# A feed-forward's gate and up products as seven block products instead of eight

## The chip, the cores and the metric

One Trainium2 chip, and of it one core. The metric is the time of the program on the device in microseconds. TensorE (the profile's PE) multiplies and accumulates in PSUM, VectorE (DVE) and ScalarE (ACT) work on elements, GpSimd (POOL) had next to no work so far, and SyncE (SP) issues DMAs.

## The reference

Three transformer layers run over 512 tokens of width 1024 in fp32. Each ends with a gated feed-forward of width 2816. The change concerns that of the third layer:

```python
u = rmsnorm(h, norm2_w[l]) * (1.0 + sc2) + sh2
ff = (jax.nn.silu(u @ w_ffn_gate[l]) * (u @ w_ffn_up[l])) @ w_ffn_down[l]
h = h + g2 * ff
```

## The kernel before

Activations are transposed: 128 features on the partitions, 512 tokens along the free axis, so that 1024 features are eight k-tiles. An fp32 product is made of three passes. Each operand is split into a high part (rounded, by a copy on ScalarE) and a low part (value minus high part, by VectorE); `mm3` issues high x high, high x low and low x high. A matmul is 128 weights wide and takes 512 tokens, or 256 where the work is done in token halves.

Weights are one stream of 128x128 tiles in the order in which they are used (`weight_plan`). Sixteen tiles are a unit of 1 MB, loaded by SP into one of `RAWBUFS` = 2 buffers `wraw` (`load_unit`, `load_ahead`); half a unit is a half-unit, split in one piece of 128x1024 into one of three pairs `whi`/`wlo` (`prep_half`). `wtile` gives a product its tile and keeps two half-units prepared ahead.

The feed-forward `ffn` (tag F2 for the third layer, 22 f-tiles of 128) works in two halves of eleven f-tiles. For each f-tile it makes gate and up (2 x 8 weight tiles, 48 matmuls), each in a PSUM bank; `act_chain` takes silu(gate) x up and splits the result into `ph`, `pl`. Then follow the eleven-tile down products of all eight outputs. In F2 the first f-tile, and the gate of the second, are made by `gemm_wide` in two token halves, because the normalized inputs `xh`, `xl` come out of `explicit_x` one half after the other. For every third k-tile `explicit_x` takes another path: the scaling on ScalarE and the low part on GpSimd (line 264).

The order of the instructions comes from a planner that runs when the kernel is built. Each stretch of work is a generator with a priority; `Core` keeps a model time for each engine, and `Core.run` always goes on with the generator that is due at TensorE's model time. Its prices (a matmul n/2400 us, a DMA by its size) only decide the order in which instructions stand in each engine's queue. On the chip every engine takes its own queue in that order and waits for what it reads and overwrites.

Of the kernel before, what the change touches and what calls it, by code (L numbers as in the profile page):

```python
# [17 lines left out]
P = 128  # L18
T = 512
# [15 lines left out]
RAWBUFS = 2  # L35
# [21 lines left out]
def weight_plan():  # L57
    tiles = []
    gains = {}

# [23 lines left out]
    def ffn(g, u, d, wide=False):  # L84
        for half in range(2):
            for f in range(half * HALF, (half + 1) * HALF):
                if wide and f == 0:
                    wide_k((g, 0), (u, 0), (g, P))
                    continue
                if not wide or f != 1:  # L90
                    form_a(g, [f])
                form_a(u, [f])
            form_a(d, range(8), nk=HALF, k0=half * HALF)

# [9 lines left out]
    while len(tiles) % UNIT:  # L104
        tiles.append(None)
# [9 lines left out]
    ffn("w_gate1", "w_up1", "w_down1")  # L115
    for what, h in ORDER_IN:
# [15 lines left out]
    ffn("w_ffn_gate_2", "w_ffn_up_2", "w_ffn_down_2", True)  # L132
    return tiles, gains


PLAN, GAINS = weight_plan()
# [25 lines left out]
class Core:  # L162
# [140 lines left out]

    def now(self):
        return self.pe_t + LAT
# [78 lines left out]
def kernel(ctx: ExitStack, tc, wst, wada, xT, vec, cst, rope, bias1, alibi, hmask, out):  # L384
# [50 lines left out]

    def raise_(hu):
# [34 lines left out]
    def load_ahead():  # L471

        while state["loaded"] < NUNITS:
            old = 2 * (state["loaded"] - RAWBUFS)
            if any(x >= state["prepped"] or highs[x] or lows[x] for x in range(max(old, 0), old + 2)):
                break
            load_unit()

    def prep_half(split=1):
# [5 lines left out]
        hi = wpool.tile([P, 1024], FR, name="whi", bufs=3)  # L485
        lo = wpool.tile([P, 1024], FR, name="wlo", bufs=3)
# [17 lines left out]
    def wtile(i, n=1, look=2, top=NHALF - 1):  # L504
        hu = i // 8
        while state["prepped"] <= min(hu + look, top):
            if state["prepped"] // 2 not in raw:
# [27 lines left out]
    def mm3(o, w, x, first, last, n=T):  # L535
        E.mm(o, w[0], x[0], first, False, n=n)
        E.mm(o, w[0], x[1], False, False, n=n)
        E.mm(o, w[1], x[0], False, last, n=n)
# [18 lines left out]
    def gemm_wide(banks, i0, hook=None, need=None, wide=False, halves=None):  # L557

        ny = len(banks)
        for t, cols in enumerate(halves or (FULL,)):  # L560
            top = (i0 + ny * KT - 1) // 8 if halves and not t else NHALF - 1
            for k in range(KT):
# [9 lines left out]
                yield  # L572

# [289 lines left out]
    def ffn(tag, pool, explicit, upd, split=False):  # L863
# [24 lines left out]
        for half in range(2):  # L888
# [14 lines left out]
            last = KT - 2 if half and split else KT  # L903
            for m in range(last):
# [485 lines left out]

    def explicit_x(bank, gain, shift, tag, t):
        c = HALVES[t]
        n = T // 2
        for k in range(KT):
            u = tmp.tile([P, n], FT, name="ut", bufs=3)
            if k % 3 == POOLK:
# [426 lines left out]
    def main():  # L1823
# [14 lines left out]
        with tc.tile_pool(name="ffn1", bufs=1) as pool:  # L1838
# [5 lines left out]
            yield from ffn("F1", pool, False, down("L2", x=False, gain2="norm_final"), split=True)  # L1844
        with tc.tile_pool(name="layer2", bufs=1) as pool:
# [4 lines left out]
        with tc.tile_pool(name="ffn2", bufs=1) as pool:  # L1850
# [3 lines left out]
            yield from ffn("F2", pool, True, down("Z", x=False, scale=mod_col(5)), split=True)  # L1854
# [79 lines left out]
```

## Time and profile before

| | us |
|---|---|
| median of 3 runs | 1929.25 (1928.06 to 1930.36) |
| the profiled execution's own time | 1928.12 |
| its span, first to last instruction | 1926.3 |
| TensorE busy | 1909.9 |
| VectorE busy | 1138.1 |
| ScalarE busy | 842.6 |
| GpSimd busy | 7.0 |

The span and all rows come from the one profiled execution. A busy time is the sum of an engine's instructions; matmuls overlap in it, so that the start-to-start distance says more than the length of one. The granted TensorE clock was 0.999 of full speed over the span.

### The profile page before, as it was taken

Reading aid. Unit: us, or ns where it says so; the run is one execution under the profiler, and the core shown is the slowest. Engines: PE = TensorE matmul, PEld = TensorE weight load, DVE = VectorE, ACT = ScalarE, POOL = GpSimd, SP = SyncE. Lnnn points to the kernel's source line nnn. Section 1 sums busy time; section 2 is a strip of 40 time slices with the busy share of each in tenths; the row PEclk is TensorE's granted clock in tenths of the full one; section 3 lists DMA queues with packets and bytes.
Section 4 is the critical chain, followed back from the end, with each engine's and each line's share of the span. In section 5 each row is a group of like instructions: output and inputs, shape, how many; then the busy total and the mean of one; then the engine's idle time right before and its main releaser. Section 6 shows DMA issues by size and latency. Waiting matters only on the chain.

```text
span 1926.3 us, 23731 instructions
## 1 busy us (share of the span) xinstructions
PE 1909.9 (99%) x9331; PEld 1593.4 (83%) x9331; DVE 1138.1 (59%) x1946; ACT 842.6 (44%) x1361; POOL 7.0 (0%) x14
## 2 busy tenths in 40 slices
PE   9999999999999999999999999999999999999998
PEld 6888888888888878888888888898888888888887
DVE  5877866655665578887543344475777563333334
ACT  4876743322333466665332233352555452212233
POOL 0000000000000000000000000000000000000000
PEclk9999999999999999999999999999999999999999
DMA  6333224544542344431322232322121222222321
GB/s 195 100 88 99 77 88 173 203 182 175 188 173 88 124 134 129 129 116 66 110 95 102 88 109 88 109 81 99 55 81 47 88 88 88 100 97 90 108 88 66
DMA packets 48303, 211.94 MB, mean 110 GB/s; under 512 B 7056, under 2 KB 10304, under 8 KB 29248
## 3 DMA queue, kind: packets, MB, share of 16 engines
q1 hardware_dynamic: 48192, 210.43, 32.5%
q8 instruction: 73, 1.20, 0.3%
q14 instruction: 38, 0.31, 0.0%
HBM read 186.26 MB, written 2.10 MB: 98 GB/s over the span
## 4 chain that ended last, share of the span: by engine, by line
PE 96%; DVE 2%; DMA 1%; ACT 1%; issue 0%; SPq 0%; POOLq 0%; POOL 0%; DVEq 0%; ACTq 0%
PE ps L229 94%; PE ps L235 2%; DMA wraw<-wst 0%; DMA h<-xT 0%; DVE wlo L260 0%; DVE xl L276 0%; ACT xh L242 0%; DVE ut L276 0%; SPq L298 0%; ACT whi L242 0%; DVE h L260 0%; ACT sqh L242 0%; ACT ut L242 0%; DVE h L276 0%; DVE e L276 0%
## 5 line engine op out<-in xcount | busy, mean ns | idle before, releaser
L229 PE MATMUL ps<-xh,whi 128*128 128x512 f32 (+1 forms) x1856 | 722.4, 389 | 3.5 <-ACT whi L242 1.8
L229 PE MATMUL ps<-xl,whi 128*128 128x512 f32 (+1 forms) x1856 | 711.4, 383 | 2.2 <-POOL xl L264 1.9
L229 PE MATMUL ps<-xh,wlo 128*128 128x512 f32 (+1 forms) x1856 | 710.8, 383 | 0.5 <-DVE wlo L260 0.5
L242 ACT ACTIVATE whi<-wraw 128x1024 fp32r<-128x1024 f32 (+1 forms) x280 | 290.8, 1039 | 603.4 <-PE ps L229 559.0
L260 DVE TENSOR_TENSOR wlo<-wraw,whi 128x1024 fp32r<-128x1024 f32 (+1 forms) x280 | 335.6, 1199 | 326.3 <-ACT whi L242 325.6
L229 PEld LDWEIGHTS ps<-xh,whi 128*128 128x128 f32 x1856 | 349.3, 188 | 73.5 <-ACT whi L242 3.3
L229 PEld LDWEIGHTS ps<-xh,wlo 128*128 128x128 f32 x1856 | 348.9, 188 | 70.3 <-DVE wlo L260 1.1
L229 PEld LDWEIGHTS ps<-xl,whi 128*128 128x128 f32 x1856 | 349.4, 188 | 69.2 <-DVE xl L276 3.0
L229 PE MATMUL ps<-ph,whi 128*128 128x512 f32 (+1 forms) x572 | 214.1, 374 | 0.0
L229 PE MATMUL ps<-pl,whi 128*128 128x512 f32 (+1 forms) x572 | 213.2, 373 | 0.0
L229 PE MATMUL ps<-ph,wlo 128*128 128x512 f32 (+1 forms) x572 | 213.2, 373 | 0.0
L229 PEld LDWEIGHTS ps<-ph,whi 128*128 128x128 f32 x572 | 107.7, 188 | 19.1
L229 PEld LDWEIGHTS ps<-ph,wlo 128*128 128x128 f32 x572 | 107.7, 188 | 18.9
L229 PEld LDWEIGHTS ps<-pl,whi 128*128 128x128 f32 x572 | 107.7, 188 | 18.8
L260 DVE TENSOR_TENSOR fu<-ps,rb 128x512 f32<-128x512 f32 x44 | 30.4, 691 | 95.8 <-PE ps L229 95.8
L260 DVE TENSOR_TENSOR h<-ps,h 128x512 f32<-128x512 f32 (+1 forms) x82 | 49.7, 621 | 60.6 <-PE ps L229 58.9
L242 ACT ACTIVATE fs<-fg 128x512 f32<-128x512 f32 x44 | 27.8, 631 | 91.1 <-DVE fg L260 91.1
L260 DVE TENSOR_TENSOR fs<-ps,fs 128x512 f32<-128x512 f32 x22 | 15.2, 692 | 70.2 <-PE ps L229 69.5
L242 ACT ACTIVATE ph<-fs 128x512 fp32r<-128x512 f32 x66 | 41.7, 632 | 28.4 <-DVE fs L260 28.4
L276 DVE SCALAR_TENSOR_TENSOR adacc<-adaw,sc,adacc 128x1024 f32<-128x1024 f32 x42 | 53.7, 1279 | 0.0
L242 ACT ACTIVATE e<-e 128x1024 f32<-128x1024 f32 (+1 forms) x48 | 41.3, 906 | 21.1 <-DVE e L269 21.0
L242 ACT ACTIVATE s<-s,md 128x256 f32<-128x256 f32 (+3 forms) x80 | 45.9, 585 | 9.9 <-DVE md L269 8.5
(211 smaller groups left out, 1976.4 us busy)
## 6 DMA issues: line engine op xcount, KB each, us to landing
wraw<-wst SPq DMA_DIRECT2D x148, 1024.0 KB, 4.8
adaw<-wada SPq DMA_DIRECT2D x48, 512.0 KB, 5.7
qhh<-hin SPq DMA_DIRECT2D x32, 128.0 KB, 2.4
rfs<-rf SPq DMA_DIRECT2D x64, 64.0 KB, 2.0
khh<-rf SPq DMA_DIRECT2D x32, 128.0 KB, 2.4
h<-xT SPq DMA_DIRECT2D x8, 256.0 KB, 5.2
kst<-hin SPq DMA_DIRECT2D x16, 128.0 KB, 2.4
kst<-qkf SPq DMA_DIRECT2D x16, 128.0 KB, 2.4
```

Source lines behind the costliest of these rows:

```text
L229: self.nc.tensor.matmul(out, lhsT, rhs, start=start, stop=stop, skip_group_check=not group)
L235: self.nc.tensor.transpose(out, in_, ident)
L242: self.nc.scalar.activation(out, in_, func, **kw)
L260: self.nc.vector.tensor_tensor(out, a, b, op)
L276: self.nc.vector.scalar_tensor_tensor(out, a, s, b, op0, op1)
```

## The change

For f-tiles 2 to 10 and 11 to 21 of F2, gate and up of one f-tile are one product of two by two blocks: the weights by rows (gate, up) and by halves of the inputs (k-tiles 0 to 3, 4 to 7), the inputs by those halves and by halves of the tokens (c1, c2). Eight block products of 4 k-tiles become seven (Strassen's scheme in Winograd's form, the up row with its sign turned), each 4 k-tiles x 3 passes of 256 tokens. Tile by tile one unit of 16 weight tiles holds `a11`, `a12` (gate) and `a21`, `a22` (up).

- The products need weight sums: S1 = a21 + a22, S3 = a21 + a11, S2 = a11 + S1, S4 = a12 + S2. GpSimd makes them with DMAs that add to their target (`add_dma`): S1 in a buffer `s1` (three of them; SP loads a21 from HBM, a DMA from HBM adds a22), the others in the raw unit itself, in place. S2 overwrites a11 and S4 overwrites a12, so these must be split first. All seven blocks (512 wide) are then split one by one, in the order of the products, into a ring of ten slots: the six halves of the three pairs and four more (`split_highs`, `split_lows`).
- The inputs need sums as well (`blocks`), once: values of the first token half by a copying and an adding DMA, differences by VectorE, then four more splits for each of four pairs of k-tiles.
- A chain of ScalarE and VectorE operations on 256 tokens (`chain`) takes partial results out of PSUM between the products.
- A raw unit is loaded again only when all seven blocks of the tile in it are split; the third raw buffer is for the whole kernel. The down weights are filled up to a whole unit.
- In F2 `explicit_x` now has one path for all k-tiles, on VectorE and ScalarE, and leaves its values in buffers for `blocks`.

```diff
-RAWBUFS = 2
+RAWBUFS = 3
...
+                if seven and f > 1:
+                    sevens.append(len(tiles) // UNIT)
...
+    def add_dma(self, out, a, sbuf=True):
+        self.nc.gpsimd.dma_start(out, a, accum_op=OP.add)
+        t = max(self.pool_t, self._ready("pool_t", [out], [a] if sbuf else [])) + 1.0
+        self.pool_t = t
+        self._done("pool_d", [out], [a] if sbuf else [], t + DMALAT + 0.7)
...
+    hi_slots = wpool.tile([P, 6, 512], FR, name="whi")
+    lo_slots = wpool.tile([P, 6, 512], FR, name="wlo")
...
+            if old >= 0 and old // 2 in sums_of:
+                break
             load_unit()
...
+            if x > hu and (any(taken[2 * state["pair"] + y] for y in range(2)) or
+                           (x // 2 not in raw and state["loaded"] > 1 and state["loaded"] - 2 in sums_of)):
+                break
...
+    def steps_of(n):
+        steps = [(x, f) for f in range(EARLY) for x in ("a11", "a12")]
+        steps += [(x, f) for x in ("s1", "s2", "s3") for f in range(EARLY)]
+        steps += [(x, f) for f in range(EARLY - 1) for x in ("a22", "s4")]
+        for f in range(EARLY, n - 1):
+            steps += [("a11", f), ("a12", f), ("s1", f), ("s2", f), ("a22", f - 1), ("s4", f - 1), ("s3", f)]
+        f = n - 1
+        steps += [("a11", f), ("a12", f), ("s1", f), ("s2", f), ("a22", f - 1), ("s3", f), ("s4", f - 1), ("a22", f),
+                  ("s4", f)]
+        return steps
...
+    def sums(u0):
...
+        E.spawn(loads(), 899)
+        yield from first(0)
+        for f in range(g["n"]):
+            u = u0 + f
+            if f + 1 < g["n"]:
+                yield from first(f + 1)
...
+            b = [raw[u][:, i * 512:(i + 1) * 512] for i in range(4)]
+            yield from got(*(f"W{u}{x}" for x in (("a11", "a12") if f else ())))
...
+            yield from add(u, b[2], b[0], "S3")
+            yield from add(u, b[0], g["s1"][u], "S2")
+            yield from add(u, b[1], b[0], "S4")
...
+    def split_highs(u0):
...
+        for i, (name, f) in enumerate(g["steps"][2:], 2):
+            u, s = u0 + f, ring[i % len(ring)]
...
+            if taken[s]:
+                yield lambda: not taken[s]
+            taken[s] = True
...
+            g["lows"].append((name, f, E.act(hi, src, AF.Copy)))
...
+    def seven(u0, name, f, out, x, fresh):
...
+        for j in range(4):
+            c = slice(j * P, (j + 1) * P)
+            a, b = yield from x(j)
+            yield from E.there(hi[:, c], lo[:, c], a, b)
+            mm3(out, (hi[:, c], lo[:, c]), (a, b), fresh and j == 0, True, T // 2, False)
+            yield
+        taken[g["slot"][name, f]] = None
...
+        def blocks(j):
+            b = [value[j][:, x, :] for x in range(2)]
+            for x in range(2):
+                yield from E.get(f"{tag}x{j + 4 * x}_0")
+                E.dma(b[x], xh[:, j + 4 * x, c1].bitcast(FT), 128, sbuf=True)
+                yield E._ready("pool_t", [b[x]], [])
+                E.add_dma(b[x], xl[:, j + 4 * x, c1].bitcast(FT))
...
+            E.stt(e, z1, ds, z0, OP.add, OP.subtract, n=n)
...
+            q = b[0]
+            d = E.add_dma(q, e)
...
+            yield E.tt(v, q, b[1], OP.subtract, n=n)
...
+        def chain(half, u, f, a, r5):
+            r = ps[:, a, c1]
+            yield from E.get(f"W{u}pa12")
...
+            d = E.act(g[:, c1], r, AF.Copy, n=n)
+            yield d
+            d = E.tt(g[:, c1], ps[:, a, c2], g[:, c1], OP.add, n=n)
+            E.set(f"W{u}c1", d)
+            yield d
+            E.act(g[:, c1], g[:, c1], AF.Silu, n=n)
+            yield from E.get(f"W{u}ps2")
+            E.set(f"W{u}c2", E.act(g[:, c2], r, AF.Copy, n=n))
+            yield from E.get(f"W{u}ps3")
+            d = E.act(v, r, AF.Copy, scale=-1.0, n=n)
...
+            for name, f in groups[u0]["steps"]:
...
+                before = {"s2": "c1", "s3": "c2", "a22": "c3", "s4": "c4"}.get(name)
+                if before:
+                    yield from E.get(f"W{u}{before}")
...
-            if k % 3 == POOLK:
+            if k % 3 == POOLK and tag != "F2":
...
-            yield from ffn("F2", pool, True, down("Z", x=False, scale=mod_col(5)), split=True)
+            yield from ffn_seven("F2", pool, True, down("Z", x=False, scale=mod_col(5)), split=True)
...
-    nc = bacc.Bacc("TRN2", target_bir_lowering=False, num_devices=1)
+    nc = bacc.Bacc("TRN2", target_bir_lowering=False, num_devices=1, dynamic_dma_scratch_size=2048)
```

`EARLY` is 2, so a group begins with two tiles side by side. The first group has 63 steps, the second 77; step i uses slot i modulo 10. The ring begins with the pair that holds the first tile's a11 and a12, then come the four extra slots, then the other two pairs, of which the next half-unit to be prepared takes the first (steps 6 and 7 modulo 10). The values of `explicit_x` are kept in the buffers that later hold `ph` and `pl`.

## Rows read from the trace of the kernel before

**Rows 1.** The page's first part: busy time, share of the span, number of instructions

```profile
span 1926.3 us, 23731 instructions
...
PE 1909.9 (99%) x9331; PEld 1593.4 (83%) x9331; DVE 1138.1 (59%) x1946; ACT 842.6 (44%) x1361; POOL 7.0 (0%) x14
```

**Rows 2.** The page's fourth part: chain that ended last, by engine, by line

```profile
PE 96%; DVE 2%; DMA 1%; ACT 1%; issue 0%; SPq 0%; POOLq 0%; POOL 0%; DVEq 0%; ACTq 0%
PE ps L229 94%; PE ps L235 2%; DMA wraw<-wst 0%; DMA h<-xT 0%; DVE wlo L260 0%; DVE xl L276 0%; ACT xh L242 0%; DVE ut L276 0%; SPq L298 0%; ACT whi L242 0%; DVE h L260 0%; ACT sqh L242 0%; ACT ut L242 0%; DVE h L276 0%; DVE e L276 0%
```

**Rows 3.** Windows over F2: length, then each engine's busy time and instructions

```profile
core 0: us, PE busy (x) PEld busy (x) DVE busy (x) ACT busy (x) POOL busy (x), PEclk, DMA share, GB/s
1546.00:1556.00 10.00, 9.50 (x71) 8.40 (x70) 9.31 (x20) 6.73 (x15) 0.78 (x1) 1.00 0.31 107
1556.00:1566.00 10.00, 9.69 (x81) 9.49 (x80) 7.34 (x21) 6.17 (x14) 1.46 (x2) 1.00 0.00 0
1566.00:1576.00 10.00, 9.57 (x62) 8.56 (x62) 7.05 (x10) 6.78 (x11) 0.88 (x1) 1.00 0.36 120
1576.00:1586.00 10.00, 10.00 (x46) 8.28 (x45) 3.74 (x4) 3.20 (x4) 0.00 (x0) 1.00 0.27 98
1586.00:1596.00 10.00, 10.00 (x46) 8.29 (x45) 3.74 (x4) 3.20 (x4) 0.00 (x0) 1.00 0.26 100
...
1800.00:1900.00 100.00, 100.00 (x446) 82.93 (x445) 37.15 (x40) 33.01 (x45) 0.00 (x0) 1.00 0.25 84
```

**Rows 4.** TensorE in order of time, 1892 to 1905 us: start, length, instruction

```profile
1892.63 0.39 PE L229 MATMUL ps<-pl,whi 128*128 128x512 f32 x1
...
1899.20 0.28 PE L229 MATMUL ps<-ph,whi 128*128 128x256 f32 x1
...
1905.19 0.28 PE L229 MATMUL ps<-ph,wlo 128*128 128x256 f32 x1
```

**Rows 5.** VectorE and ScalarE in order of time, 1587 to 1599 us

```profile
1587.73 1.06 ACT L242 ACTIVATE whi<-wraw 128x1024 fp32r<-128x1024 f32 x1 [3.84 <-PE ps L229]
1588.03 0.69 DVE L260 TENSOR_TENSOR fs<-ps,fs 128x512 f32<-128x512 f32 x1 [3.36 <-PE ps L229]
1588.76 0.63 ACT L242 ACTIVATE ph<-fs 128x512 fp32r<-128x512 f32 x1
1589.97 0.68 DVE L260 TENSOR_TENSOR pl<-fs,ph 128x512 fp32r<-128x512 f32 x1
1594.33 1.23 DVE L260 TENSOR_TENSOR wlo<-wraw,whi 128x1024 fp32r<-128x1024 f32 x1 [3.67 <-ACT whi L242]
1598.91 0.69 DVE L260 TENSOR_TENSOR fs<-ps,fs 128x512 f32<-128x512 f32 x1 [3.36 <-PE ps L229]
```

**Rows 6.** VectorE and ScalarE in order of time, pieces of 256 tokens, 1561 to 1563 us

```profile
1561.11 0.48 DVE L276 SCALAR_TENSOR_TENSOR xl<-ut,mod,xh 128x256 fp32r<-128x256 f32 x1 [0.19 <-ACT xh L242]
1561.52 0.42 DVE L260 TENSOR_TENSOR ut<-ps,h 128x256 f32<-128x256 f32 x1
1562.03 0.60 ACT L242 ACTIVATE ut<-ut,mod,gv 128x256 f32<-128x256 f32 x1 [0.95 <-DVE ut L260]
1562.66 0.42 ACT L242 ACTIVATE xh<-ut 128x256 fp32r<-128x256 f32 x1
```

**Rows 7.** The page's sixth part, DMA issues: KB of one, median us to landing

```profile
adaw<-wada SPq DMA_DIRECT2D x48, 512.0 KB, 5.7
...
out<-h SPq DMA_DIRECT2D x8, 256.0 KB, 2.2
...
khh<-khh SPq DMA_DIRECT2D x8, 128.0 KB, 5.6
al<-alibi SPq DMA_DIRECT2D x4, 256.0 KB, 5.1
```

**Rows 8.** SP's queue in order of time, the shortest issues

```profile
10.65 0.33 SPq L298 DMA_DIRECT2D wraw<-wst  x1
```

**Rows 9.** GpSimd in order of time, the longest of its subtractions

```profile
1567.26 0.88 POOL L264 TENSOR_TENSOR xl<-ut,xh 128x256 fp32r<-128x256 f32 x1 [3.30 <-ACT xh L242]
```

**Rows 10.** The chain that ended last, in order of time, 1564 to 1580 us

```profile
1564.24 0.40 DVE ut L276
1564.65 0.02 issue
1564.67 0.51 ACT xh L242
1565.18 0.95 ACT whi L242
1566.13 0.55 ACT ut L242
1566.68 0.02 issue
1566.70 0.43 ACT xh L242
...
1567.24 0.92 POOLq L1929
1568.15 0.04 issue
1568.19 12.02 PE ps L229 x64
```

More of the change, by code (lines that the diff above doesn't have):

```diff
@@ L82, in out_proj, with fill, ffn @@
                     tiles.append((name, k * P, m * P))
-    def ffn(g, u, d, wide=False):
+    def fill():
+        while len(tiles) % UNIT:
+            tiles.append(None)
+    def ffn(g, u, d, wide=False, seven=False):
         for half in range(2):
@@ L93, in ffn @@
             form_a(d, range(8), nk=HALF, k0=half * HALF)
+            if seven:
+                fill()
     for p in range(8):
@@ L103, in weight_plan @@
     ffn("w_gate0", "w_up0", "w_down0")
-    while len(tiles) % UNIT:
-        tiles.append(None)
+    fill()
     for p in range(8):
@@ L115, in weight_plan @@
     ffn("w_gate1", "w_up1", "w_down1")
+    fill()
     for what, h in ORDER_IN:
@@ L434 @@
     quiet, by_hand = [], {0, 1}
+    hi_slots = wpool.tile([P, 6, 512], FR, name="whi")
+    lo_slots = wpool.tile([P, 6, 512], FR, name="wlo")
+    slots = [(hi_slots[:, i, :], lo_slots[:, i, :]) for i in range(6)]
+    taken = [None] * 6
+    state["pair"] = 0
+    sums_of = set(SEVENS)
     def raise_(hu):
@@ new lines, in open_group, with block, begin_group @@
+    def open_group(u):
+        n = 1
+        while u + n in SEVENS and n < HALF:
+            n += 1
+        for x in range(n):
+            group_of[u + x] = u
+        groups[u] = dict(n=n, steps=steps_of(n), s1={}, lows=[], slot={}, pool=None, ring=None)
+    def block(u, name):
+        g = groups[group_of[u]]
+        if name == "s1":
+            return g["s1"][u]
+        o = BLOCK[name] * 512
+        return raw[u][:, o:o + 512]
+    def begin_group(u, pool, more):
+        yield lambda: u in raw
+        if u not in group_of:
+            open_group(u)
+        g = groups[u]
+        g["pool"] = pool
+        E.spawn(sums(u), 901)
+        yield lambda: state["prepped"] == 2 * u + 1
+        first = 2 * ((state["pair"] - 1) % 3)
+        g["ring"] = [first, first + 1, *more, *((first + x) % 6 for x in range(2, 6))]
+        for x in range(6):
+            taken[x] = True
+        for x in range(2):
+            g["slot"]["a11" if x == 0 else "a12", 0] = first + x
+        for x in range(state["prepped"], 2 * (u + g["n"])):
+            highs[x] = lows[x] = []
+        state["prepped"] = 2 * (u + g["n"])
+        E.spawn(split_highs(u), 902)
+        E.spawn(split_lows(u), 903)
@@ new lines, in split_lows @@
+    def split_lows(u0):
+        g = groups[u0]
+        left = {}
+        for name, f in g["steps"][2:]:
+            left[f] = left.get(f, 0) + 1
+        for _ in g["steps"][2:]:
+            if not g["lows"]:
+                yield lambda: g["lows"]
+            name, f, d = g["lows"].pop(0)
+            u = u0 + f
+            hi, lo = slots[g["slot"][name, f]]
+            t = max(E.dve_t - SLACKD, d)
+            if t > E.pe_t:
+                yield t
+            E.set(f"W{u}{name}")
+            E.set(f"W{u}{name}x", E.tt(lo, block(u, name), hi.bitcast(FT), OP.subtract))
+            left[f] -= 1
+            if not left[f]:
+                sums_of.discard(u)
+                load_ahead()
@@ new lines, in seven @@
+    def seven(u0, name, f, out, x, fresh):
+        g, u = groups[u0], u0 + f
+        if (name, f) in g["steps"][:2]:
+            hi, lo = wtile(u * UNIT + BLOCK[name] * 4, 4, look=0)
+        else:
+            yield from E.get(f"W{u}{name}x")
+            hi, lo = slots[g["slot"][name, f]]
+        for j in range(4):
[5 more added lines that the diff above has]
+        taken[g["slot"][name, f]] = None
@@ L903, in ffn @@
             last = KT - 2 if half and split else KT
+            for m in range(last):
+                b = yield from E.alloc()
+                hook = (lambda k: E.set(f"{tag}d{k}", E.now())) if m == KT - 1 else None
+                yield from gemm_a(b[0], take(HALF), lambda k: (ph[k], pl[k]), nk=HALF,
+                                  need=f"{tag}p{half}_" if m == 0 else None, hook=hook)
+                E.spawn(upd(m, b[0], half), 3)
+            if last == KT:
+                continue
+            i = take((KT - last) * HALF)
```

219 lines of the change are left out of this document (208 added, 11 removed).

## Prediction

> **What bounds the kernel now.** I read the page's first part, the chain that ended last, and then a table of windows over the last feed-forward (F2, from about 1548 us on). TensorE is busy 99% of the span [rows 1], and 96% of the chain is TensorE [rows 2]. The windows say what lies beside it in the gate and up products: in 1586 to 1596 us TensorE is full, VectorE has 3.74 of 10 us, ScalarE 3.20, GpSimd nothing, and the DMA engines are busy 0.26 [rows 3]. So a matmul that goes away is time gained, until one of those four fills up; how near each comes is the question.
>
> The next view is TensorE's order in time where the kernel itself goes from 512 to 256 columns. From 1892.63 to 1899.20 us stand 29 matmuls of 512 columns: 6.57/29 = 0.2266 us each. From 1899.20 to 1905.19 us stand 50 of 256: 5.99/50 = 0.1198 us [rows 4]. Half the columns cost more than half the time (0.1133). An f-tile (16 weight tiles, three passes, 48 matmuls) is then 48 x 0.2266 = 10.88 us, and VectorE's product of gate and up returns after 1598.91 - 1588.03 = 10.88 us [rows 5]. Nothing else sets the pace there.
>
> **The products.** Twenty f-tiles go from 48 wide matmuls to 7 x 4 x 3 = 84 narrow ones: 84 x 0.1198 = 10.06 us against 10.88, 0.81 us each, **-16.2 us** in all. The columns alone fall by one eighth (1.36 us a tile, 27 us); the step of a narrow matmul takes the rest. The Trainium skill (TensorE: Matmul & The Clock Gate, Back-to-back issue gap) gives N / 2.4 + 2.5 ns; by it a tile would go from 10.36 to 9.17 us and the sum would be 23.7 us. The rows differ from it by 11 to 13 ns a matmul, and the rows decide.
>
> **Splitting the weights.** Four blocks of 512 become seven. ScalarE: 7 x 0.63 for the high parts, 0.63 for the result's, five pieces of 256 at 0.42 to 0.60 [rows 5, 6], about 7.3 us in 10.06. VectorE: 7 x 0.68, 0.68, five pieces of 0.42 to 0.48, about 7.7 us. Both stay under TensorE's 10.06 us, which hides them: **0 us**. If something held VectorE for 2.4 us in every tile, the cover would be gone, and each tenth of a microsecond beyond would cost 2 us over twenty tiles.
>
> **Sums of the weights.** GpSimd, idle until now [rows 1], issues four accumulating DMAs of 256 KB a tile: S1 of the next tile, then S3, S2, S4. S2 overwrites what S3 reads, and S4 reads what S2 writes, so each of the two waits stands at the head of GpSimd's queue, with the next tile's S1 and S3 behind it. With T from its turn to its landing and i for an issue that waits for nothing, the queue goes round in 2T + 2i. The trace has no accumulating DMA. The nearest transfers: 256 KB with nothing beside it lands in 2.2 us; 256 KB and 128 KB behind other loads in 5.1 and 5.6; 512 KB among its like in 5.7 [rows 7]. An issue: 0.33 us on SP at the least [rows 8], 0.88 if it takes GpSimd as long as its longest subtraction [rows 9]. Bounds: 2 x 2.2 + 2 x 0.33 = 5.1 us and 2 x 5.7 + 2 x 0.88 = 13.2 us. Loads will run beside these transfers for about a third of the time, so I take T = 2.2 + (5.6 - 2.2)/3 = 3.3, and 0.7 for reading the target as well as the source (256 KB at the rate below): 4.0; with i = 0.8 the round is 9.6 us, under 10.06: **0 us**, by a margin of 0.5. At the upper end it costs (13.2 - 10.06) x 20 = 63 us, less the lead. The lead is some 4 us in each of the two groups: with ten slots a tile's first block can be split nine steps ahead, S2's product comes three steps after that block, and of these 12 x 1.44 = 17.2 us two splits of 1.3 and two T of 4.0 take 10.6, the queue's other two issues and the fixed order of the splits part of the rest. So +55 us at worst.
>
> **DMA engines.** A tile's 1.05 MB now uses 0.26 to 0.27 of 10 us, 2.7 us of all sixteen engines [rows 3]. The new tile loads 1.25 times that (the second half of the up weights twice), 3.4 us, and adds as much again as one load. If an added byte costs the engines one copied byte, the tile uses 6.1 us; twice, 8.8; three times, 11.5 against 10.06. I take twice, the target being read too: hidden below the 10.06 us, +21 us at three times (1.44 x 20 less the 8 us of lead). The Trainium skill (DMA: Bandwidth & Descriptors, Issuing engines are not separate DMA queues) says that DMAs from any engine run on the same sixteen and interleave. With engines of their own the adds would leave 3.4 us here and the rival of full engines would fall away; no row has two queues at work, and I count them on the same sixteen.
>
> **The start of F2.** The sums of the inputs are new: per pair of k-tiles three additions and four low halves on VectorE (3 x 0.46 + 4 x 0.45 = 3.2 us, 12.7 in all), four copies on ScalarE, and 8 plain and 12 accumulating DMAs. The normalization's third-tile path leaves ScalarE and GpSimd for VectorE: four pieces, 0.55 us more each. VectorE already has 9.31, 7.34 and 7.05 us in the three windows from 1546 us on, and TensorE waits there for the inputs [rows 3, 10]. The moved pieces take away ScalarE, GpSimd and their hand-overs (3.5 us from the ready sum at 1564.67 to TensorE's start at 1568.19 [rows 10]), about what VectorE's extra 2.2 us give back. Until S2's input is wanted, some 14 us after the second half of the inputs is there plus the blocks before it, VectorE has nearly as much to do as time, and a third of the upper bound is my choice: **+3 us** (-1 to +8.6: the hand-overs alone, or all 12.7 + 2.2 us less the 6.3 that VectorE has idle in those windows).
>
> **The down projections.** During a group nothing prefetches the down weights, as the slots are taken; the first 1,024-wide piece is split when the group ends. In the second group the last of the 77 steps uses a slot of that very pair (77th step, ring of ten, seventh slot), so ScalarE's 1.06 and VectorE's 1.23 us [rows 5] come after TensorE's last read: 2.2 us. In the first group (63 steps) the pair is free, but queued behind the last tile's chain: 1 us. **+3.2 us** (0, if the low part hides under the first two matmuls and the queue is short, to 4.6, both groups in full). Nothing else hides it; before, the split lay two pieces ahead.
>
> **Hand-overs in PSUM.** S2's product overwrites the bank part that ScalarE must have copied (0.42 us); the S1 product, 12 x 0.1198 = 1.44 us, is the cover. If the copy queues behind a split (0.63) it still fits; behind two (1.68) each tile loses 0.24: **+1 us** (0 to 4.8).
>
> **Elsewhere.** A third raw buffer lets SP load earlier through the whole kernel, and the padding adds 1 MB. In the steady stretch loads use a quarter of the engines [rows 3], which hides the padding, and SP's queue has 0% of the chain [rows 2]: 0 (-2 to +2, a tenth of a percent of the span, which such a share can hide).
>
> Sum: -16.2 + 3 + 3.2 + 1 = -9.0 us on a profiled execution of 1928.12 us, 1919.1. The median of the runs shown stands 1.1 us above that execution: **1920.3 us**.
>
> **Rivals.** *The queue of sums sets the pace* (slower): place, GpSimd's queue at S2 and S4; for it, transfers that share the engines take 5.1 to 5.7 us [rows 7]; against it, the free one takes 2.2. With T = 5.1 the round is 11.8: 1.74 x 20 - 8 = +27, so 1947 us. It decides from the point where 20 (2T + 2i - 10.06) - 8 = 9, a round of 10.9 us or T = 4.7. The Trainium skill (DMA: Bandwidth & Descriptors, Rules for kernel authors) says that a DMA which reads what another wrote must wait for its semaphore; by that rule T counts twice, as above. The same page's formula (Anatomy of one DMA), 2.0 us plus bytes over 436 GB/s, would give T = 2.6 and a round of 6.8 us, as an estimate, for a plain copy. *The DMA engines fill up*: at three bytes for one, 1941 us; the shares before leave 0.73 free, which speaks against it. *The gain is eaten*: the start at +8.6, the down projections at +4.6 and the hand-overs at +4.8 give +18.0 against -16.2, 1931 us, no change; for it, two engines at three quarters and VectorE's full windows. *No stall at all*: -16.2 alone, 1913 us.
>
> **How the numbers follow.** My forecast has 0.52, no stall 0.08, the gain eaten 0.14, the queue 0.17, the DMA engines 0.09. What this measurement can tell from no change is 0.2%, 3.9 us. Faster: the first two, 0.60. Slower: queue and engines, save 0.01 near the turning point, 0.25. The same: 0.15. The range takes in no stall (less 2 for the rest of the kernel) and the queue at T = 5.1: 1911 to 1948. The forecast's own range is 1915 to 1925.
>
> **What would show it.** Right: in the windows of the groups 84 matmuls every 10.1 us, narrow steps at 0.12 us, ScalarE and VectorE near 0.75, GpSimd's sums landing before the split that reads them. Wrong: TensorE idle in every tile, released by ScalarE or VectorE behind a DMA (the queue); landings that lengthen with the engines' share near 1 (the engines); idle only where a group begins or ends (terms of start and down projections mis-sized). A first F2 product much later than now would condemn the third buffer or the moved normalization.

## The result, and the profile after

The changed kernel takes **2017.78 us** (median of 4 runs, 2017.08 to 2018.56) against 1928.65 us (4 runs, 1926.09 to 1930.36): ratio 1.0463, 95% interval 1.0445 to 1.0482, **slower by 4.6%** where I forecast 1920.3. The profiled execution has a span of 2016.7 us, 90.4 more than before.

The page's first part, which answers to [rows 1]: TensorE is busy 96% of a longer span, GpSimd 4%.

```profile
PE 1930.0 (96%) x10051; PEld 1643.7 (82%) x10051; DVE 1210.6 (60%) x2160; ACT 904.9 (45%) x1551; POOL 84.8 (4%) x102
```

Next the stages of the last feed-forward, as windows cut where TensorE's operands change. The columns are those of [rows 3]; the lines are the changed kernel's end of the wide products, first group (9 tiles), first down projection, second group (11 tiles), and the rest.

```profile
1571.40:1584.40 13.00, 10.16 (x41) 8.31 (x40) 12.38 (x29) 9.92 (x23) 6.44 (x8) 0.74 0.76 143
1584.40:1717.50 133.10, 101.87 (x757) 100.04 (x755) 59.19 (x114) 52.91 (x114) 25.48 (x29) 0.91 0.61 143
1717.50:1778.90 61.40, 60.84 (x264) 49.59 (x265) 23.18 (x26) 15.08 (x18) 4.99 (x7) 1.00 0.43 135
1778.90:1943.10 164.20, 130.29 (x925) 127.64 (x923) 71.38 (x136) 63.91 (x136) 33.71 (x39) 0.86 0.64 147
1943.10:2016.70 73.60, 64.23 (x350) 55.15 (x350) 31.67 (x55) 26.00 (x43) 0.00 (x0) 0.96 0.21 72
```

And the same stages of the kernel before, with its nine and eleven wide tiles:

```profile
1571.40:1576.80 5.40, 5.40 (x26) 4.48 (x25) 2.69 (x4) 2.76 (x5) 0.00 (x0) 1.00 0.28 76
1576.80:1674.80 98.00, 98.00 (x434) 81.13 (x433) 33.70 (x36) 28.47 (x36) 0.00 (x0) 1.00 0.28 100
1674.80:1734.60 59.80, 59.80 (x265) 49.54 (x264) 19.75 (x20) 12.21 (x12) 0.00 (x0) 1.00 0.27 95
1734.60:1854.30 119.70, 119.70 (x529) 99.10 (x529) 40.63 (x43) 34.08 (x43) 0.00 (x0) 1.00 0.28 97
1854.30:1926.30 72.00, 63.45 (x351) 55.18 (x349) 29.34 (x52) 24.81 (x41) 0.00 (x0) 0.97 0.21 74
```

The reader is to see where the 90 us lie: +7.6 ahead of the first group, **+35.1 and +44.5 in the two groups**, +1.6 and +1.6 in the down projections. Up to the last pieces of the normalized input nothing differs: TensorE's wait for a low part of the second half ends within a microsecond of before (1567.37 against 1568.19 us). TensorE, which was full in both groups, now is not: the nine tiles hold 756 narrow matmuls, 756 x 0.1198 = 90.6 us; TensorE is busy 101.9 and idle 31.2. In the second group 924 matmuls are 110.7 us; it is busy 130.3 and idle 33.9. So of the 96 us beyond the bare products 65 are idle time and some 31 are matmuls that ran slower than 0.1198: the granted clock is 0.91 and 0.86 there, against 1.00 before. All of the first group's idle time lies in eight waits, about one for each tile, for partial sums `fs` out of PSUM (us in total, times, longest):

```profile
PE ps L238 <- ACT fs L251: 17.9, 4, 6.1
PE ps L238 <- DVE fs L269: 13.2, 4, 4.7
```

Then GpSimd in order of time over one tile and the beginning of the next. `wraw<-s` is S2, `s<-wst` S1, and of the two `wraw<-wraw` the first is S4, the second S3 of the next tile. The length is the issue's own.

```profile
1604.60 0.86 POOL L315 DMA_DIRECT2D wraw<-wraw  x1 [3.94 <-DMA wraw<-s]
1605.14 1.22 POOL L315 DMA_DIRECT2D s<-wst  x1
1605.67 1.57 POOL L315 DMA_DIRECT2D wraw<-wraw  x1
1615.65 0.86 POOL L315 DMA_DIRECT2D wraw<-s  x1 [8.40 <-issue]
1620.55 0.86 POOL L315 DMA_DIRECT2D wraw<-wraw  x1 [4.04 <-issue]
1621.10 1.21 POOL L315 DMA_DIRECT2D s<-wst  x1
1621.63 1.58 POOL L315 DMA_DIRECT2D wraw<-wraw  x1
1631.80 0.87 POOL L315 DMA_DIRECT2D wraw<-s  x1 [8.59 <-DMA wraw<-wraw]
```

From one S2 to the next are 16.15 us here (14.8 on the mean: 133.1/9). Between them stand two waits of different size: about 4 us from S2 to S4, and over 8 from S3 to the next S2. S3 is issued third: S4 and S1 are on their way when it starts. And SP issues the 1 MB load of a later tile right behind the three, which then runs beside them:

```profile
1606.95 0.33 SPq L307 DMA_DIRECT2D wraw<-wst  x1
```

The landings of 1600 to 1680 us (median from issue) say the same; S2 is the one that goes alone:

```profile
wraw<-wraw POOLq DMA_DIRECT2D x10, 256.0 KB, 6.7
wraw<-s POOLq DMA_DIRECT2D x6, 256.0 KB, 3.3
s<-wst POOLq DMA_DIRECT2D x5, 256.0 KB, 8.2
```

The three that were issued from 1604.60 on landed after 3.9, 6.8 and 9.4 us: one after another, some 3.3 us apart. How this reaches TensorE is seen on ScalarE and TensorE in order of time:

```profile
1613.06 0.38 ACT L251 ACTIVATE fs<-ps 128x256 f32<-128x256 f32 x1 [1.77 <-PE ps L238]
1619.91 2.19 ACT L251 ACTIVATE whx<-wraw 128x512 fp32r<-128x512 f32 x4 [6.47 <-DMA wraw<-s]
1622.01 1.13 ACT L251 ACTIVATE whi<-wraw 128x512 fp32r<-128x512 f32 x2
```
```profile
1622.25 0.28 PE L238 MATMUL ps<-xh,wlo 128*128 128x256 f32 x1
1627.20 0.58 PE L238 MATMUL ps<-th,whx 128*128 128x256 f32 x1 [4.67 <-DVE fs L269]
1627.58 0.42 PE L238 MATMUL ps<-tl,whx 128*128 128x256 f32 x1
1627.80 0.42 PE L238 MATMUL ps<-th,wlx 128*128 128x256 f32 x1
```

ScalarE waits 6.47 us for S2's landing (1615.65 + 4.2), with six more splits and the copies out of PSUM queued behind; then TensorE waits 4.67 us for a sum that VectorE could make only after ScalarE's late copy. The name at the wait is VectorE, the cause is the DMA two engines behind it. After the wait TensorE's steps are 0.21 us, not 0.12: the granted clock is 0.50 of full in 1626 to 1630 us, which is the 1.2 GHz level, after 4.7 us of idling.

### The profile page after: what moved, and what is told of

The parts are those of the page before. It is cut to its first block, busy times and chain, and to the rows that moved or that the text cites. A ratio compares the mean times of both kernels' runs of the same rounds, so it can differ in the third digit from the quotient of the medians.

```text
span 2016.7 us, 25922 instructions
## 1 busy us (share of the span) xinstructions
PE 1930.0 (96%) x10051; PEld 1643.7 (82%) x10051; DVE 1210.6 (60%) x2160; ACT 904.9 (45%) x1551; POOL 84.8 (4%) x102
## 3 DMA queue, kind: packets, MB, share of 16 engines
q8 instruction: 79, 1.29, 0.3%
## 5 line engine op out<-in xcount | busy, mean ns | idle before, releaser
L238 PE MATMUL ps<-xh,whi 128*128 128x512 f32 (+1 forms) x1712 | 650.8, 380 | 2.7 <-ACT xh L251 1.4
L238 PE MATMUL ps<-xl,whi 128*128 128x512 f32 (+1 forms) x1712 | 639.9, 374 | 6.4 <-DVE xl L285 3.6
L238 PE MATMUL ps<-xh,wlo 128*128 128x512 f32 (+1 forms) x1712 | 638.4, 373 | 0.8 <-DVE wlo L269 0.5
L269 DVE TENSOR_TENSOR wlo<-wraw,whi 128x1024 fp32r<-128x1024 f32 (+2 forms) x312 | 334.2, 1080 | 318.9 <-ACT whi L251 318.4
L251 ACT ACTIVATE whi<-wraw 128x1024 fp32r<-128x1024 f32 (+2 forms) x312 | 289.7, 942 | 503.9 <-PE ps L238 419.7
L238 PEld LDWEIGHTS ps<-xh,wlo 128*128 128x128 f32 x1712 | 325.1, 190 | 58.5 <-DVE wlo L269 1.0
L269 DVE TENSOR_TENSOR fu<-ps,rb 128x512 f32<-128x512 f32 x44 | 30.4, 690 | 95.9 <-PE ps L238 95.9
L238 PE MATMUL ps<-th,whi 128*128 128x256 f32 x156 | 50.1, 321 | 32.2 <-ACT fs L251 17.3
L238 PEld LDWEIGHTS ps<-th,whi 128*128 128x128 f32 x156 | 34.7, 223 | 34.2 <-ACT fs L251 18.3
L238 PE MATMUL ps<-th,whx 128*128 128x256 f32 x84 | 29.2, 347 | 31.5 <-DVE fs L269 15.8
L269 DVE TENSOR_TENSOR wlx<-wraw,whx 128x512 fp32r<-128x512 f32 x46 | 30.4, 684 | 46.1 <-ACT whx L251 45.9
```

Source lines behind the costliest of these rows:

```text
L238: self.nc.tensor.matmul(out, lhsT, rhs, start=start, stop=stop, skip_group_check=not group)
L251: self.nc.scalar.activation(out, in_, func, **kw)
L269: self.nc.vector.tensor_tensor(out, a, b, op)
```

## The experiments

All are single runs beside a run of the kernel before unless a number of runs is given; the runs of the kernel before lay within 1926.1 and 1930.7 us, so a difference of under some 5 us between two single runs says little here. In the texts on record S1 to S4 are the four sums of a tile's weights; a22, s2 and so on are TensorE's block products.

**The adding DMA by itself.** Nothing of the kernel is left; accumulating DMAs stand between barriers, with and without company.

> A kernel with DMAs alone, none of the network: adding DMAs of 256 KB issued by GpSimd one at a time, three and eight in a row, plain copies of the same queue and of SP's, larger and smaller rows, with 1 MB loads beside, with VectorE busy; then additions by GpSimd itself. Theory A (one queue's adding transfers drain one after another, each some 3.3 us, whatever else runs): one add lands in 3 to 4 us, three in about 10, eight in about 26, loads beside change little. Rival B (the adds are quick, loads on the shared engines make them late): one add 3 to 4, eight alone in 8 to 13, and much more only with loads beside. If descriptors on GpSimd are the limit, plain copies of its queue are as slow as adds, or VectorE's work lengthens them.

DMA queues of three adds in 11 us, and of one plain copy of the same 256 KB in 6 us (packets, MB, share of the 16 engines):

```profile
q0 software_dynamic: 432, 0.79, 42.3%
```
```profile
q0 software_dynamic: 80, 0.26, 11.4%
```

An add takes 0.423 x 11/3 = 1.55 us of all sixteen engines, a copy 0.114 x 6 = 0.68: 2.3 copies. Alone, an add lands in 3.3 us. Three in a row with nothing beside them landed, each from its own issue, after:

```profile
DMA to landing us min/median/max: 3.3/4.3/5.2
```

Eight in a row took 73.7% of 17 us, 12.5 us, again 1.57 each, so theory A (some 26) falls and rival B holds: beside four loads of 1 MB the median landing of eight adds was 16.7 us, against 6.8 without. Eight plain copies on the same queue landed after 2.3 to 3.9 us, and VectorE's work beside eight adds lengthened nothing (3.3 to 9.6 us against 3.3 to 9.8), so descriptors on GpSimd are not the limit. So a third place in the queue alone makes 5.2 us of 3.3; the 9.4 in the changed kernel need the loads as well. An issue took 0.86 us on GpSimd, a copy's 0.57. A 512-wide addition on GpSimd itself took 1.23 us, and 1.57 with VectorE subtractions beside it (four in 4.92 and in 6.27 us).

**No accumulating DMAs: GpSimd adds (e1).**

```diff
-            E.set(f"W{u}{flag}", E.add_dma(out, x))
+            E.set(f"W{u}{flag}", E.ptt(out, out, x, OP.add))
...
```

> The same seven products, all four weight sums made by additions on GpSimd in place of DMAs (and S1 from the raw unit, without its own load). If the adding DMAs are the whole of the loss (A and B), TensorE sets the pace again, 10.06 us a tile, plus what the starts cost (8 to 10 us in all): 1919 to 1930 us. If splits, PSUM hand-overs or the chain on ScalarE and VectorE set the pace (rival D), it stays above 1980 us.

1988.99 us (1985.5 to 1990.29, 4 runs), ratio 1.0309 (1.0291 to 1.0326). A third of the loss goes; 61 us stay though no accumulating DMA of weights is left. The number is rival D's, but the trace shows another wait: S1 of the next tile stands at the head of GpSimd's queue and waits 6.8 to 8.5 us in tile after tile for the next unit's load, with the three sums of the present tile behind it. It is an order again, with another transfer at its head; what it is worth by itself, e5 shows.

**Another order of the four adds (e2).**

```diff
-            if f + 1 < g["n"]:
-                yield from first(f + 1)
...
-            yield from add(u, b[2], b[0], "S3")
             yield from add(u, b[0], g["s1"][u], "S2")
+            if f + 1 < g["n"]:
+                yield from first(f + 1)
+                nb = yield from ready(u + 1)
+                yield from add(u + 1, nb[2], nb[0], "S3")
             yield from add(u, b[1], b[0], "S4")
```

> The four adds of a tile in another order: S2, then S1 and S3 of the next tile, then S4, so that S2 never stands behind three adds and the queue is never empty. A: the queue still drains at some 3.3 us an add, 13.2 us a tile instead of 14.8, so 1980 to 1990 us. Rival C (only the order of the waits is to blame, an add alone lands in time): 10.1 to 10.6 us a tile, 1925 to 1940 us.

1956.27 us, between the two ranges. The same four DMAs, and 61.5 of 89 us are gone: S2 no longer stands behind an S3 that is third in the queue. Part of what is left is seen on the DMA queues of 1600 to 1680 us:

```profile
q0 software_dynamic: 3694, 6.72, 49.5%
q1 hardware_dynamic: 1541, 8.16, 30.4%
```

An add is 0.495 x 80/(6.72/0.262) = 1.54 us of sixteen engines, a loaded megabyte 0.304 x 80/8.16 = 2.98. A tile's four adds and 1.31 MB make 6.2 + 3.9 = 10.1 us, as much as TensorE's 10.06. (In the changed kernel the engines' share is 0.61 of 14.8 us, 9.0 us a tile: there they are not full.) The other part is on GpSimd, where S3 of the next tile now waits at the head of the queue for that tile's load, 2.3 to 4.2 us in five tiles of this stretch, with S4 behind it:

```profile
1602.73 0.86 POOL L315 DMA_DIRECT2D wraw<-wraw  x1 [4.22 <-DMA wraw<-wst]
```

**Fewer loads (e3: in the changed kernel; e4: with the other order).** Twelve of the twenty units reuse the raw unit of three before.

```diff
+        if u in sums_of and u in REUSED:
+            t = raw[u - 3]
+            E.dma(t[:, 0:P], wst[u, :, 0:P], 1024.0)
...
```

> 12 of the 20 block-product tiles reuse a raw unit with 64 KB loaded in place of 1 MB; it leaves out those weights. A: these tiles still take 13.5 to 15 us, 2005 us or more in all. B: they go to 10 to 11 us, so 12 x 4 = 48 us less, about 1970 us.

1983.51 us: 34 of the 89, between the two theories. The queue of three adds stays; it only drains faster. S3, third in it, lands after 6.3 and 6.1 us (issues at 1604.76 and 1628.91) where it took 9.4 to 9.8 in the changed kernel, and S2 follows S2 after 12.2 us on the mean of five rounds from 1599.8 us on, where the changed kernel takes 15.8. Two of them:

```profile
1623.88 0.87 POOL L315 DMA_DIRECT2D wraw<-s  x1 [5.24 <-DMA wraw<-wraw]
1635.76 0.86 POOL L315 DMA_DIRECT2D wraw<-s  x1 [5.27 <-issue]
```

So of the 5.7 us by which a round exceeds TensorE's 10.06, 3.6 go with the loads and 2.1 stay with the queue.

> The changed kernel with its adds in the order S2 of a tile, then S1 and S3 of the next, then S4 of the tile, and with 12 of the 20 units' loads cut from 1 MB to 64 KB (those tiles compute with the weights of the unit three before them: the weights of 12 tiles are left out). With the order alone the kernel took 1956.3 us, 28 over the kernel before. Theory A, what is left there is the 16 DMA engines, which the loads and the adds together fill to 0.9 and over: with most loads gone, the twelve tiles fall from about 11.4 us to about 10.1, so 1938 to 1943. Theory B, what is left is the hand-over in PSUM behind bursts of splits and the slow clock after each pause: at most 4 us, 1952 to 1957.

1933.3 us, better than theory A's figure. Two windows of e4 in the first group:

```profile
1610.00:1630.00 20.00, 20.00 (x169) 20.00 (x168) 15.42 (x29) 12.69 (x27) 7.04 (x8) 1.00 0.87 170
1630.00:1650.00 20.00, 20.00 (x168) 19.96 (x168) 14.27 (x26) 12.68 (x26) 7.02 (x8) 1.00 0.72 129
```

168.5 matmuls in 20 us: a tile in 10 us, TensorE full, with VectorE at 0.74 and ScalarE at 0.63. So the product step of the prediction holds where no wait interferes. The 23 us between e2 and e4 hang on the loads; whether by the engines that they fill or by S3's wait for the load, no run separates, as fewer loads take away both.

**GpSimd's sums with S1 last (e5), and without bursts of splits (e6, e7).**

```diff
-            if f + 1 < g["n"]:
-                yield from first(f + 1)
...
             yield from add(u, b[1], b[0], "S4")
+            if f + 1 < g["n"]:
+                yield from first(f + 1)
```

> All four sums by GpSimd additions, as in the run before of that kind (1989.0 us), but S1 of the next tile stands behind S3, S2 and S4 of this one, and not before them. Theory A (the wait of S1 for the next unit's load holds up the three sums behind it; the loads wait for the splits, the splits for the sums, a ring): with the ring cut a tile falls from 13.5 to 10.1-11 us, 1920 to 1940. Theory B (the planner's bursts of splits on ScalarE and VectorE delay the copy out of PSUM whatever the sums do): 1980 to 1990.

1977.51 us, which is neither: cutting the ring is worth 11.5 us. Another thing shows, on GpSimd, VectorE and TensorE in order of time:

```profile
1640.55 1.74 POOL L273 TENSOR_TENSOR s<-wraw 128x512 f32<-128x512 f32 x1
1642.37 1.59 POOL L273 TENSOR_TENSOR wraw<-wraw 128x512 f32<-128x512 f32 x1
```
```profile
1641.06 1.78 DVE L269 TENSOR_TENSOR pl<-fs,ph 128x512 fp32r<-128x512 f32 x1
1642.76 1.75 DVE L269 TENSOR_TENSOR wlo<-wraw,whi 128x512 fp32r<-128x512 f32 x1
1644.43 0.41 DVE L269 TENSOR_TENSOR fs<-ps,fs 128x256 f32<-128x256 f32 x1
```
```profile
1644.90 0.39 PE L238 MATMUL ps<-th,whi 128*128 128x256 f32 x1 [1.93 <-DVE fs L269]
```

GpSimd's addition (1.29 us by itself) and VectorE's subtraction (0.69) take 1.6 to 1.8 us each while they run side by side, with no adding DMA of weights about, and TensorE waits 1.93 us for the sum that stands behind them.

The Trainium skill (GPSIMD Engine Reference, Key points) says that GpSimd shares its SBUF interfaces with VectorE and contends with it where VectorE's instruction has two SBUF inputs; both of these have two, and the trace agrees.

```diff
-            t = max(E.act_t - SLACK, E._ready("act_t", [hi], [src]))
+            t = max(E.act_t - 0.6, E._ready("act_t", [hi], [src]))
```

> As the run before it, and the planner may put a split on ScalarE's queue only 0.6 us ahead of ScalarE's own time, not 5 us, so that no burst of splits can stand ahead of the copies out of PSUM. Theory A (the ring of loads and sums is all): within 3 us of the run before. Theory B (bursts): 10 to 50 us faster than the run before, as far as that lies over 1925; the waits of TensorE for fs fall from some 3.5 us per tile to under 1.

1979.31 us. And the same edit on e2:

> The changed kernel with its adds in the other order (1956.3 us) and the planner's slack for ScalarE's splits of 0.6 us in place of 5. Theory A (the DMA engines set the pace there): 1953 to 1959. Theory B (bursts of splits ahead of the copies out of PSUM): 1930 to 1945.

1960.86 us. Neither is faster than the run that it changes: bursts of splits, my own theory after e1, fall.

**Half by DMA, half by GpSimd (e8), and one step of TensorE moved (e9 to e12).**

```diff
+            E.set(f"W{u}{flag}", E.add_dma(out, x) if flag == "S3" else E.ptt(out, out, x, OP.add))
...
-  ("a11", f), ("a12", f), ("s1", f), ("s2", f), ("a22", f - 1), ("s4", f - 1), ("s3", f)
+  ("a11", f), ("a12", f), ("s1", f), ("a22", f - 1), ("s2", f), ("s4", f - 1), ("s3", f)
```

> S2 and S4 by GpSimd additions, S1 and S3 by accumulating DMAs that are issued a tile early, behind S4 of the tile before. Theory A (two prices: GpSimd's additions slow VectorE where they run beside it, accumulating DMAs fill the engines; each is borne when halved): the DMA share falls from 0.9-1.0 to about 0.7, no three adds stand in a row, tiles of 10.1 to 10.7 us, 1925 to 1940. Theory B (the hand-over in PSUM costs some 2 us per tile whichever way the sums are made, since the copies out of PSUM stand behind splits on their queues): 1950 to 1970.

1947.79 us, between the two ranges.

> As the run before it, with one step of TensorE moved: a22 of the tile before stands ahead of s2 and not behind it, so that two products (2.9 us), not one (1.44 us), cover the sum out of PSUM that s2 waits for. Theory A (hand-over costs nothing once the sums are early): within 3 us of the run before. Theory B (the hand-over): 10 to 40 us faster than the run before, with TensorE's waits for fs gone.

1966.49 us: **slower** by 19, which neither theory allowed. GpSimd in order of time shows a ring again:

```profile
1608.89 1.29 POOL L273 TENSOR_TENSOR wraw<-wraw,s 128x512 f32<-128x512 f32 x1 [7.58 <-DMA wraw<-wraw]
1610.26 1.27 POOL L273 TENSOR_TENSOR wraw<-wraw 128x512 f32<-128x512 f32 x1
1611.47 0.87 POOL L315 DMA_DIRECT2D s<-wst  x1
1612.06 1.19 POOL L315 DMA_DIRECT2D wraw<-wraw  x1
1620.55 1.28 POOL L273 TENSOR_TENSOR wraw<-wraw,s 128x512 f32<-128x512 f32 x1 [7.31 <-DMA wraw<-wraw]
```

S2, S4, S1's issue, S3's issue, and S3's landing 8.5 us later releases the next S2: 11.7 us a turn.

> All sums on GpSimd, S1 late (1977.5 us, where GpSimd's additions and VectorE's pl and wlo run side by side at 1.6 to 1.8 us each and c1's addition comes 1.9 us late once a tile), with a22 of the tile before moved ahead of s2. If the late c1 is what costs there (some 2 us and the slow clock behind it, in nearly every tile), the time falls by 25 to 45 us, to 1932 to 1952; if the sums themselves or the loads are late, it stays over 1970.

1958.07 us, 19 less than e5 and 6 above the range.

> All sums by accumulating DMAs in the other order (1956.3 us), with a22 of the tile before moved ahead of s2, which gives s2's weights and c1 1.44 us more. If the DMA engines set the pace there, 1952 to 1958; if the hand-over or S2's lateness does, 1935 to 1948.

1947.24 us, 9 less than e2. So where the sums are early, the hand-over in PSUM does cost, or S2's split comes late: the move gives both 1.44 us more. In the changed kernel itself neither shows:

> The changed kernel with one step of TensorE moved and nothing else: a22 of the tile before ahead of s2. Theory A (S2's sum stands third in the adding queue, and the pace of 14.8 us a tile is the queue's): 2005 to 2022, as before the move. Theory B (the hand-over in PSUM holds a good part of the 89 us): 1985 to 2000.

2022.0 us, no gain: the queue of sums covers it.

**The ring taken apart (e13 to e15).** S1 is issued two tiles ahead, S3 between S2 and S4 of the tile before.

```diff
             yield from add(u, b[0], g["s1"][u], "S2")
+            if f + 1 < g["n"]:
+                nb = yield from ready(u + 1)
+                yield from add(u + 1, nb[2], nb[0], "S3")
             yield from add(u, b[1], b[0], "S4")
+            if f + 2 < g["n"]:
+                yield from first(f + 2)
```

> The hybrid (S2 and S4 on GpSimd, S1 and S3 by accumulating DMAs, 1947.8 us) with S1 issued two tiles ahead and S3 between S2 and S4 of the tile before, so that S1 and S3 never stand one right behind the other ahead of S2. If the ring S4, S1, S3, S2 (some 12 us a turn, seen in the hybrid with the moved step) held it: 1933 to 1943. If it was the start and the hand-over: within 3 us of 1947.8.

1942.31 us, within the ring's range.

> As e13, with a22 of the tile before ahead of s2. In the hybrid this move cost 19 us, and its trace shows the ring of S4, S1, S3 and S2 at 12.1 us a turn. Theory A (the ring): without it the move costs nothing or gains, 1925 to 1938. Theory B (the move itself is bad where GpSimd makes S2): 1955 to 1970.

1931.89 us: the move of a22, which had cost 19 us in the hybrid with the ring, now gains 10. So the ring is what made the move cost; why it turned more slowly with the move is not shown.

> S1 alone by an accumulating DMA, two tiles ahead; S2, S3 and S4 by GpSimd additions; the moved step. Engines: one add a tile (1.5 us of all sixteen beside 3.4 of loads). If the DMA engines still cost in e14, this is faster than e14 by 3 to 8 us; if GpSimd's additions beside VectorE cost more (1.75 us for a subtraction of 0.69), slower by 3 to 10.

1936.86 us, 5 more than e14. By the traces 3.7 of it lie in the two groups (95.9 and 114.5 us against 93.3 and 113.3): with three sums on GpSimd, its price beside VectorE seems to outweigh what the DMA engines get back, by single runs.

**The start (e16, e17).** The first group's splits and its first sum wait in the planner for the last of the normalized input.

```diff
         ring = g["ring"]
+        if u0 == SEVENS[0]:
+            yield from E.get(*(f"F2x{k}_1" for k in range(KT)))
...
```

In e14 the start stands so, on VectorE and TensorE in order of time:

```profile
1573.39 1.22 DVE L269 TENSOR_TENSOR wlo<-wraw,whi 128x1024 fp32r<-128x1024 f32 x1
1574.52 0.68 DVE L269 TENSOR_TENSOR wlx<-wraw,whx 128x512 fp32r<-128x512 f32 x1
1575.12 1.48 DVE L269 TENSOR_TENSOR d<-b 128x256 f32<-128x256 f32 x1
1576.53 2.47 DVE L269 TENSOR_TENSOR wlx<-wraw,whx 128x512 fp32r<-128x512 f32 x1
1578.92 0.47 DVE L285 SCALAR_TENSOR_TENSOR xl<-c,mod,xh 128x256 fp32r<-128x256 f32 x1
```
```profile
1579.45 0.58 PE L238 MATMUL ps<-xl,whi 128*128 128x256 f32 x1 [4.33 <-DVE xl L285]
```

Two of VectorE's rows are long, 1.48 and 2.47 us for what takes 0.41 and 0.68 in the changed kernel: GpSimd's additions run beside them (1574.69 to 1578.43). So this wait is partly the order and partly GpSimd's price.

> As e14 (1931.9 us), and the first group's splits and its first sum wait in the planner until all of the second half's normalized input is split, so that the last xl stands ahead of them on VectorE's queue. In e14 TensorE waited 4.33 us for that xl, after 1.38 us for its xh, and then ran some 4 us at half the clock; after that it has only 1.4 us of waits to the first down projection. If the start is what is left: 5 to 8 us faster than e14, 1924 to 1927, a little faster than the kernel before. If VectorE's work at the start is merely moved and is late afterwards for the first narrow products: within 2 us of e14.

1929.31 us (11 runs, 1927.33 to 1932.98) against 1928.24 (15 runs): ratio 1.0009, interval 1.0000 to 1.0017. The first narrow product starts at 1581.99, not 1587.71, 5.7 us earlier; the first group then takes 99.3 us, not 93.3, with waits of 2.10 and 0.74 us for VectorE at 1593 and 1596, among its deferred work, and a granted clock of 0.97. By the first down projection (1681.26 against 1681.05) all of the gain is given back; the 2.6 us between the two times are no more than e16's own runs differ.

> The changed kernel with that move at the start alone. Theory A (the queue of the sums sets the pace of each tile, and what is won at the start is given back, since the sums of the first tiles come no earlier): 2013 to 2020. Theory B (the start's 4 to 5 us are lost for themselves): 2010 to 2014.

2018.72 us (4 runs, 2017.26 to 2019.95): 1.8 us won at the start, 1.4 given back in the first group: theory A.

The stages side by side, in us, each from its first matmul to the next stage's (TensorE in order of time; the last column is the span's):

| kernel | first narrow product at | 9 tiles | down | 11 tiles | rest | span |
|---|---|---|---|---|---|---|
| before | (wide) 1576.85 | 97.95 | 59.84 | 119.68 | 71.98 | 1926.3 |
| changed | 1584.39 | 133.14 | 61.38 | 164.19 | 73.6 | 2016.7 |
| e2 order | 1584.46 | 108.02 | 61.40 | 127.04 | 73.6 | 1954.5 |
| e4 order, fewer loads | 1582.96 | 92.98 | 61.40 | 118.94 | 75.1 | 1931.4 |
| e14 hybrid | 1587.71 | 93.34 | 60.51 | 113.32 | 75.1 | 1930.0 |
| e16 hybrid, start | 1581.99 | 99.27 | 60.51 | 112.83 | 73.5 | 1928.1 |

No version here beats the kernel before beyond what the measurement can tell. The best, e14 and e16, win 11 and 5.5 us of the 16.2 in the groups and pay them back at the start, the down projections and the rest.

## Why the prediction was wrong, step by step

**The step that failed: "Sums of the weights: 0 us".** The round of GpSimd's queue was taken as 2T + 2i with one T of 4.0 us for both waits, 9.6 us in all. For the wait behind S2, which goes alone, T is right: 4.2 us. For the wait behind S3 it measured 9.4 to 9.8 us, for two reasons. S4 and S1 are issued 1.1 and 0.5 us before it on the same adding queue; "with the next tile's S1 and S3 behind it" stands in my text, yet I let S3 land as if alone. And the loads run beside these three adds in every tile, not "for about a third of the time". The third of three landed in 5.2 us with nothing beside it (m1), in 6.1 and 6.3 with the loads cut (e3). By measured numbers the round is 4.2 + 0.7 to S4's issue, 1.1 to S3's, 9.5 to its landing, 0.7 to the next S2: 16.2, against 16.15 in the trace. My upper bound of 13.2 us took 5.7 from [rows 7] for both waits and so did not hold it either. e2, which only changes the order, gives back 61.5 of 89 us: this step, with the clock that hangs on it, is shown as the larger part. The loads' share in it is shown by e3, 34 us with twelve of twenty loads cut; the two overlap and can't be added.

**"DMA engines: 0 us" was mis-sized.** I took an added byte as two copied ones and 8.8 us a tile. It measured 2.3, and a loaded megabyte beside the adds 2.98 us, not 2.6: 10.1 us, at the edge of the 10.06. In the changed kernel the engines are not full (0.61 of 14.8 us); once the order is mended, 23 us hang on the loads (e2 against e4), by the engines or by S3's wait for the load.

**The clock was in no term.** Some 31 of the 96 us are matmuls at less than full clock, after waits of 2.7 to 6.2 us, though not after each (the clock stayed at 1.00 after 3.26 us at 1637). In this kernel a stall cost its length and then more.

**The products** were right: 0.12 us a step, and 10 us a tile in e4 where TensorE doesn't wait. One reading there was off, without effect: both rows lie 11 ns above the formula quoted beside them, not 11 to 13. **Splitting the weights**: VectorE 14.84 and ScalarE 12.68 of 20 us in e4, 7.4 and 6.3 a tile against my 7.7 and 7.3; hidden as said.

**The start** was +7.5, not +3: inside my bound of 8.6. The work that I counted is there, but I spread it over the idle time, whereas the queues put the new sums and the first group's splits ahead of the last low and high parts: TensorE's waits there grow by some 4 us (the longest 1.46 for xl and 1.38 for xh), and after them the granted clock is 0.50 in 1574 to 1580 us, which costs another 2.4. Moving the first group's splits alone wins 1.8 of it (e17), and e16 shows that it only moves the cost.

**The down projections** were +3.2. They measured +1.6 and +1.6 from their first matmul on, and waits of 0.16 and 1.08 us for ScalarE's split just ahead of it lie in the groups' windows: some 4.4 us, under my bound of 4.6, the second group's share the larger, as I had it. **Elsewhere** 0: right, the third raw buffer changes nothing up to the start of F2's second half.

**Hand-overs in PSUM**, +1: nothing in the changed kernel (e12), as a longer wait lies over it. With the sums early the move is worth 9 to 19 us (e2 to e11, e13 to e14, e5 to e10), beyond my 4.8: there the cover of 1.44 us was too thin, for the copy or for S2's split.

**The rival** "the queue of sums sets the pace" had the right engine, the right two waits and the right sign, with a chance of 0.17; at 1947 us it was sized by the same equal T and fell short by 71 us. Its test, TensorE idle in every tile behind ScalarE or VectorE behind a DMA, is what the trace shows. The Trainium skill (DMA: Bandwidth & Descriptors, Anatomy of one DMA) would give 2.6 us for T, as an estimate by its formula for a copy; the lone copy landed in 2.3 and the lone add in 3.3, and neither tells the third in the queue. The same page's rule that queues of all engines share the sixteen (Issuing engines are not separate DMA queues) agrees: with fewer loads from SP's queue S3 on GpSimd's lands in 6.1 and 6.3 us, not 9.4 to 9.8 (e3).

What stays open: in e2 and e11, how much the full DMA engines cost and how much S3's wait for the load; in e9, why the ring turned more slowly. In e14 the 5.4 us beyond 20 tiles of 10.06 are no slower pace in every tile: they lie in a few waits, of which the longest are 1.24 us early in the first group, 0.47 in the last tile of each, and 1.08 for the down weights' split.

## What to carry to other kernels

When several transfers are issued on one queue, give each its own landing time, by its place in the queue and by what else is loaded meanwhile, and read the period of the ring from the one that is waited for, not from a lone transfer. Put first what releases a wait, and count a stall at its length plus the matmuls that run at the lower clock behind it. An engine that was idle is not free: here GpSimd's additions slowed VectorE (0.69 to 1.75 us), and its DMAs took 6.2 us a tile of the engines that bring the weights.

## What the runs showed of the hardware

- An accumulating DMA of 256 KB takes 1.55 us of all sixteen engines against 0.68 for a copy, lands in 3.3 us alone; three in a row landed 3.3, 4.3 and 5.2 us after their issues with nothing beside them (m1), and 3.9, 6.8 and 9.4 beside loads (changed kernel).
- GpSimd's 512-wide addition took 1.29 us and VectorE's subtraction 0.69; side by side both took 1.6 to 1.8 us (e5).
- After 4.7 us of idling TensorE's granted clock was 0.50 in the windows 1626 to 1630 us and its 256-column steps 0.21 us; a tile earlier, after 2.97 us of waiting, the steps were so from 1611.5 to 1615 us, at a granted clock of 0.51.
